# The last pair ahead of the first inverse's products, and the bonus taken out of PSUM by ScalarE, in an SGU / RWKV-7 trunk

## The chip, the cores and the metric

The kernel runs on one core of one Trainium2 chip. The core has a matrix engine (TensorE, "PE" in the profile, with its weight loads shown apart as "PEld"), VectorE ("DVE"), ScalarE ("ACT"), GpSimd ("POOL") and SyncE ("SP"). Each engine takes its instructions from a queue of its own, in order. The metric is the device time of one execution in microseconds (us): the median of several runs of the kernel. One more execution was profiled; it gives the trace.

## The reference: what is computed

The input is 512 tokens of 1024 channels. Two residual layers follow each other. Layer 0 mixes tokens with a spatial-gating unit (SGU), layer 1 with RWKV-7 time mixing; each is followed by a gated convolutional FFN of width 2816, and a last RMSNorm ends the program. The change lies in layer 1 alone, whose mixer is, cut to what matters:

```python
r, k, v = xr @ w_r, xk @ w_k, xv @ w_v
kk = normalised(k * k_k) ; k = k * (1 + (a - 1) * k_a)
# per head (16 heads of 64), for each token t:
#   S = S diag(w_t) + (S a_t) b_t^T + v_t k_t^T ;  y_t = S r_t
y = wkv7_scan(r, decay, k, v, -kk, kk * a)
y = group_norm(y) * ln_w + ln_b
bonus = sum(r * k * r_k, per head) * v
out = ((y + bonus) * g) @ w_o
```

## The kernel before, in words

**Layout.** Activations lie with channels on the 128 partitions and the 512 tokens along the free dimension; 1024 channels are eight such tiles, which for the RWKV layer are called *pairs* (a tile holds two heads). Every dense product in fp32 is made of three products of rounded halves (mm3, L325 to L327): each k-tile costs three matmuls of 128x512.

**The chunked scan.** The recurrence is cut into eight chunks of 64 tokens. For each chunk and head a 64x64 triangular system must be inverted, and the matrices that enter it are made beforehand. The work of the layer is therefore split into streams, written as Python generators, each of which emits a bit of work and yields:

- `projections` (L808): the dense products for k, then for v, eight tiles each. In this part of the program one step makes two k-tiles of one output tile, that is six dense matmuls. Behind each v tile a generator `value` (L859) does the rest for it: it centres v through the PE (L868) and writes it out (L873, L874), and it makes the bonus: a product of r*k with a block matrix that holds r_k (L883), a multiplication by v (L885), and a ScalarE pass that adds the bias ln_b (L886). The product's PSUM bank is one of two of the tag "mm", which the dense products of the same stage also use (for the last tiles it is "aux"), and the bank is free again when L885 has read it.
- `pairs`: for each of the eight pairs, decay and operands (VectorE and ScalarE), and then `products` (L959): small matmuls into the banks "aux" and "us" (L973, L988), masked by VectorE (L977), copied by ScalarE (L978, L991) and written to DRAM for the scan. The first half of a pair's chunks is one step, the second half with L988 another.
- `invert(g)` (L1027): the inverses for pairs 4g to 4g+3, all chunks at once. ScalarE (for g = 1 partly VectorE) copies the 32x32 diagonal blocks (L1044, L1046), VectorE transposes them (L1051), solves row by row (rows j = 1 to 30, two dependent VectorE instructions each, L1069 and L1070; two rows to a step), and transposes the result twice, to z and to y. Then the off-diagonal blocks: first-stage products from z on the PE (L1090), copies of y by ScalarE (L1098), copies of the products (L1103), second-stage products from y (L1093) and their copies (L1105).
- `scan(g)`: the chunks in order, each a chain of small matmuls and copies (L1301 to L1329), with `finish` for the group norm, which adds the bonus from rt, and `gate` (L1203), which multiplies by the gate (L1209) and splits the result for the output projection.

**What sets the order.** The streams are woven by hand. `weave(main, side, fill, rate, lag, side_rate)` steps `main`; after each step it draws the dense stream `fill` at `rate` steps per main step, and the inverse (`side`) at `side_rate`. The tuple RATES holds these numbers per stage. `issue_after(ins)` orders what is emitted inside behind `ins` on the same engine; `step(gen, engines)` steps a generator behind the last instruction so far on the engines named. Everything that is not ordered this way or by data may be placed earlier in an engine's queue by the compiler.

Around the change the order of emission is: a stage in which the pairs 4 to 6 and the first half of pair 7 are the main stream, with the first inverse at 2.2 steps per main step (RATES[1]); then these lines:

```python
load(0, 0)
ahead = invert(1)
next(ahead)
self.weave(main, inv, fill, *RATES[4], ktiles=STEPS[1])
for _ in inv:
    next(fill)
    self.step(ahead, (mybir.EngineType.PE,))
```

that is, the second inverse's first input copies, the rest of pair 7 together with the first inverse, and what is left of that inverse with one dense step and one step of the second inverse each. Then comes `scan(0)`, with the second inverse as side stream. In `invert`, one dense step is drawn between the transposes z and y of the first inverse.

Of the kernel before, what the change touches and what calls it, by code (L numbers as in the profile page):

```python
# [12 lines left out]
F32 = mybir.dt.float32  # L13
F32R = mybir.dt.float32r
AF = mybir.ActivationFunctionType
ALU = mybir.AluOpType
# [4 lines left out]
P = 128  # L21
D = 1024
KT = 8
T = 512
# [5 lines left out]
GN_EPS = 64e-5  # L30
C1 = -0.5 * math.exp(-0.5)

RATES = ((1.9, 2), (1.9, 6, 2.2), (0.66, 2, 1.15), (0.72, 2), (1.2, 6, 2.2))
LEAD = 1
WB = 4
FIRST0, WAIT, STEPS = 1, 1, (2, 2, 2, 2)
# [108 lines left out]
class Emit:  # L145
# [622 lines left out]
    def rwkv_main(self, r, ctx, gain):  # L768
        nc, tc, A = self.nc, self.tc, self.A
        V, S, G = nc.vector, nc.scalar, nc.gpsimd  # L770
# [5 lines left out]
        ip = r.ip  # L776
# [31 lines left out]
        def projections():  # L808

            load = Ahead([lambda n=n, m=m: self.parts(n, m) for n in PARTS for m in range(KT)])  # L810

            def key(m, a):
                while m >= NKEY and m - NKEY not in used:
                    yield
                ks[m] = tmp("key", NKEY, T)
                S.copy(ks[m], a)

            for m in range(KT - 2):
                a = self.acc("mm")
                yield from self.dense_steps(a, load.take(), r.xk)  # L820
                yield from key(m, a)
                yield

            ws = [load.take(), load.take(False)]
            accs = [self.acc("mm") for _ in range(2)]
            xv = []
            for k in range(KT):
                for j in range(2):
                    self.mm3(accs[j], self.wcols(ws[j], k * P, P), r.xk[k], k == 0, k == KT - 1)
                while len(xv) < min(k + 3, KT):  # L830
                    xv.append(r.mix(3, len(xv)))
                if k == 4:
                    load.fetch()
                yield
            for j in range(2):
                yield from key(KT - 2 + j, accs[j])
            late = iter(())
            for m in range(KT):
                a = self.acc("mm")
                w = load.take()  # L840
                if m == KT - 2:
                    ga["w"] = load_gate(0)
                for n, _ in enumerate(self.dense_steps(a, w, xv)):
                    yield
                    next(late, None)
                    if m == KT - 1 and n == 0:
                        gw[0] = gate_weights(ga["w"])
                        ga["parts"] = self.gate_parts()
                    if m == KT - 1 and len(gx) < 2:
                        gx.append(gate_mix(len(gx)))  # L850
                for _ in late:
                    yield
                v = ip.tile([P, T], F32, tag="v", bufs=1, name=self.uid("v"))
                S.copy(v, a)
                late = value(m, v)
            next(late)
            tail.append(late)

        def value(m, v):  # L859
            g, i = divmod(m, 4)  # L860

            def bank():
                return self.acc("mm" if len(done) < KT else "aux")

            vt = ip.tile([P, NCH, C], F32, tag="vt", bufs=1, name=self.uid("vt"))
            q = bank()
            for b in range(4):
                nc.tensor.matmul(q[:, b * P:(b + 1) * P], v[:, b * P:(b + 1) * P], self.c("center", P),  # L868
                                 start=True, stop=True)
            q4 = q.rearrange("p (b h f) -> p b h f", b=4, h=2)  # L870
            for hd in range(2):
                for par in range(2):
                    S.copy(vt[H[1 - hd], par::2, :], q4[H[par], :, hd, :])  # L873
            nc.sync.dma_start(vtd[:, :, m].rearrange("c p f -> p c f"), vt)  # L874
            yield
            yield

            while m not in done:
                yield
            wb = ip.tile([P, P], F32, tag="wb", bufs=1, name=self.uid("wb"))  # L880
            S.activation(wb, self.c("bones", P), AF.Copy, scale=self.p("r_k", m))
            q = bank()
            nc.tensor.matmul(q, wb, rt[g][:, i, :], start=True, stop=True)  # L883
            b = rt[g][:, i, :]
            V.tensor_tensor(b, q, v, ALU.mult)  # L885
            S.activation(b, b, AF.Identity, bias=self.p("ln_b", m))  # L886
            vdone.add(m)
            yield

# [137 lines left out]
        def invert(g):  # L1027
# [9 lines left out]

            x = blocks("ix")
            pr = ip.tile([P, 272], F32, tag="pr", bufs=1, name=self.uid("pr"))
            cut = 24 * g  # L1040
            for us in (slice(0, cut), slice(cut, 32))[1 - g:]:
                for rows, cols in Q:
                    if us.start and g == 1:
# [5 lines left out]
            def turn(out, src):  # L1049
                for bs in [slice(n, n + 8) for n in range(0, 32, 8)] if g == 1 else [slice(0, 32)]:  # L1050
                    V.transpose(out[:, bs], src[:, bs])  # L1051
# [6 lines left out]
            for j in range(1, 31):  # L1058
# [6 lines left out]
                else:  # L1065
                    a = tt[:, j, j + 1:32].unsqueeze(1).to_broadcast([P, j, ni])
                    b = tt[:, 0:j, j].unsqueeze(2).to_broadcast([P, j, ni])
                    q = pr[:, 0:ni * j].rearrange("p (c i) -> p c i", i=ni)
# [4 lines left out]

            z, y = blocks("ix"), blocks("li")
            turn(z.rearrange("p u t -> p t u"), tt)
            if g == 0:
                next(fill)
            turn(y.rearrange("p u t -> p t u"), tt.rearrange("p s t -> p t s"))
            yield
            off, own = blocks("off"), iter(Q)  # L1080
            for i in range(2):
# [22 lines left out]
                        else:  # L1104
                            S.copy(tg[b0, us, 32:64], ps[b0])  # L1105

        gx, tail = [], []

        def gate_mix(k):
            with ExitStack() as behind:  # L1110
# [92 lines left out]
        def gate(g, i, ts, q=None):  # L1203

            if q is None:
                q = self.acc("aux")[:, 0:ts.stop - ts.start]
                opening(g, i, ts, q)
            o = rt[g][:, i, ts]
            V.tensor_tensor(o, o, q, ALU.mult)  # L1209
            while len(outs[g]) <= i:  # L1210
                outs[g].append(tuple(self.xr.tile([P, T], F32R, tag=t, bufs=10, name=self.uid(t)) for t in ("mxh", "mxl")))
            oh, ol = (x[:, ts] for x in outs[g][i])
            S.copy(oh, o)
            V.tensor_tensor(ol, o, oh.bitcast(F32), ALU.subtract)
# [16 lines left out]
        def load(g, c):  # L1231
            while 4 * g + 3 not in vdone:
                next(fill)

            ps = slice(4 * g, 4 * g + 4)
            if g == c == 0:
                st = [t for _ in range(2) for t in (self.xr.tile([P, T], F32, tag=tag, bufs=10, name=self.uid(tag))
                                                    for tag in ("mxh", "mxl"))]
                bt = scratch("ss").rearrange("p (i a f) -> p i a f", i=4, a=2)
                vu = scratch("rb").rearrange("p (a i f) -> p a i f", a=2, i=4)  # L1240
                for i in range(4):
                    nc.sync.dma_start(st[i][:, 0:RW], std[g][c, :, i])
            else:
                t = tile_([P, 4 * RW], "st", SCAN)
                st = [t[:, RW * i:RW * i + RW] for i in range(4)]
                nc.sync.dma_start(t, std[g][c].rearrange("p i t -> p (i t)"))
                n = c % 2
                if n == 0 or g == 0 and c == 1:
                    two[:] = tile_([P, 2, 4, 2, C], "cbt", 2), tile_([P, 2, 2, 4, C], "vu", 2)
                    cs = slice(c, c + 2 - n)  # L1250
                    for hd in range(2):
                        nc.sync.dma_start(two[1][H[1 - hd], n:, hd], vtd[cs, H[1 - hd], ps].rearrange("c p i f -> p c i f"))
                    nc.sync.dma_start(two[0][:, n:].rearrange("p c i a f -> p c (i a f)"),
                                      btd[cs, :, ps].rearrange("c p i a f -> p c (i a f)"))
                bt, vu = (t[:, n] for t in two)
            for hd in range(2):
                if g == c == 0:
                    nc.sync.dma_start(vu[H[1 - hd], hd], vtd[c, H[1 - hd], ps])
                if c == 0:
                    G.memset(vu[H[hd], hd], 0.0)  # L1260
            if g == c == 0:
                nc.sync.dma_start(bt, btd[c][:, ps])
            chunks[g, c] = st, bt, vu
# [157 lines left out]
        main = pairs()  # L1421
# [3 lines left out]
            pass  # L1425
        self.weave(until(main, lambda: KT - 2 in done), inv, fill, *RATES[1], ktiles=STEPS[1])
        load(0, 0)
        ahead = invert(1)
        next(ahead)
        self.weave(main, inv, fill, *RATES[4], ktiles=STEPS[1])  # L1430
        for _ in inv:
            next(fill)
            self.step(ahead, (mybir.EngineType.PE,))
        ctx.close()
        ep = ctx.enter_context(tc.tile_pool(name="scan", bufs=1))
        inv = ahead
# [88 lines left out]
```

## Time and profile before

| | |
|---|---|
| median of 3 runs | 1244.42 us (1243.08 to 1244.78) |
| the profiled execution | 1245.55 us, of it 1243.7 us span |
| PE busy | 1226.8 us (99%), 7535 matmuls |
| PEld busy | 1000.2 us (80%) |
| VectorE busy | 851.1 us (68%) |
| ScalarE busy | 633.1 us (51%) |
| GpSimd busy | 81.4 us (7%) |
| mean granted TensorE clock | 0.996 of full speed |

The span is the time from the first to the last recorded instruction; the execution's own time is 1.85 us longer. The profile's page lists the engines' busy time, busy shares over 40 slices with the granted clock of the PE (PEclk), and the costliest groups of instructions. The trace behind it can be asked for a time line of an engine, for who waited for whom, and for busy times and clock by stretches. In a row of the time line stand the start, the duration, the engine, the line of the kernel, the operation, output<-input and the count; in square brackets behind it the engine's idle time before it and what ended it. Matmuls overlap, so a matmul's duration is longer than the distance to the next start.

### The profile page before, as it was taken

Reading aid. Unit: us, or ns where it says so; the run is one execution under the profiler, and the core shown is the slowest. Engines: PE = TensorE matmul, PEld = TensorE weight load, DVE = VectorE, ACT = ScalarE, POOL = GpSimd, SP = SyncE. Lnnn points to the kernel's source line nnn. Section 1 sums busy time; section 2 is a strip of 40 time slices with the busy share of each in tenths; the row PEclk is TensorE's granted clock in tenths of the full one; section 3 lists DMA queues with packets and bytes.
Section 4 is the critical chain, followed back from the end, with each engine's and each line's share of the span. In section 5 each row is a group of like instructions: output and inputs, shape, how many; then the busy total and the mean of one; then the engine's idle time right before and its main releaser. Section 6 shows DMA issues by size and latency. Waiting matters only on the chain.

```text
span 1243.7 us, 19411 instructions
## 1 busy us (share of the span) xinstructions
PE 1226.8 (99%) x7535; PEld 1000.2 (80%) x7535; DVE 851.1 (68%) x1418; ACT 633.1 (51%) x1089; POOL 81.4 (7%) x106
## 2 busy tenths in 40 slices
PE   9999999999999999999999999999999999999997
PEld 6878888888888888877887777778888888888886
DVE  5566578888876454675899698776777777872323
ACT  6544455555554343466787667424544444543232
POOL 1100200000000001000000013222000000000000
PEclk9999999999999999999999899999999999999999
DMA  7232457887556776326888797654223223333332
GB/s 273 94 105 82 132 180 246 246 249 241 192 172 193 220 226 196 109 81 182 220 242 237 188 280 233 219 171 135 85 102 102 90 97 102 97 88 104 97 93 81
DMA packets 125133, 201.65 MB, mean 162 GB/s; under 512 B 39857, under 2 KB 63153, under 8 KB 125041
## 3 DMA queue, kind: packets, MB, share of 16 engines
q10 hardware_dynamic: 38976, 112.87, 29.5%
q1 hardware_dynamic: 86064, 87.54, 22.6%
q8 instruction: 59, 0.97, 0.3%
q14 instruction: 34, 0.27, 0.1%
HBM read 152.93 MB, written 47.45 MB: 161 GB/s over the span
## 4 chain that ended last, share of the span: by engine, by line
PE 91%; DVE 4%; DMA 3%; ACT 1%; issue 0%; SPq 0%; POOL 0%; DVEq 0%; POOLq 0%; ACTq 0%
PE mm L325 9%; PE mm L327 9%; PE mm L326 9%; PE aux L325 6%; PE aux L326 6%; PE aux L327 6%; PE e L325 6%; PE e L326 6%; PE us L325 6%; PE e L327 6%; PE us L327 6%; PE us L326 6%; PE us L1314 1%; PE aux L973 1%; PE aux L988 1%; PE us L1321 1%
## 5 line engine op out<-in xcount | busy, mean ns | idle before, releaser
L237 ACT CAST w<-w 128x512 fp32r<-128x512 f32 x340 | 206.5, 611 | 359.8 <-PE aux L327 92.6
L238 DVE TENSOR_TENSOR w<-w,w 128x512 fp32r<-128x512 f32 x340 | 230.5, 680 | 180.2 <-ACT w L237 179.6
L325 PE MATMUL mm<-mxh,w 128*128 128x512 f32 x408 | 167.9, 412 | 2.7 <-DVE rt L885 2.6
L327 PE MATMUL mm<-mxh,w 128*128 128x512 f32 x408 | 161.1, 395 | 0.0
L326 PE MATMUL mm<-mxl,w 128*128 128x512 f32 x408 | 160.6, 394 | 0.0
L325 PEld LDWEIGHTS mm<-mxh,w 128*128 128x128 f32 x408 | 77.0, 189 | 22.8 <-DVE rt L885 3.3
L327 PEld LDWEIGHTS mm<-mxh,w 128*128 128x128 f32 x408 | 77.0, 189 | 17.1 <-issue 0.8
L326 PEld LDWEIGHTS mm<-mxl,w 128*128 128x128 f32 x408 | 77.1, 189 | 16.2 <-issue 1.7
L575 ACT ACTIVATE cv<-z,par 128x512 f32<-128x512 f32 x88 | 71.7, 817 | 26.5 <-DVE z L573 21.2
L325 PE MATMUL aux<-mxh,w 128*128 128x512 f32 x216 | 84.5, 391 | 0.0
L325 PE MATMUL us<-mxh,w 128*128 128x512 f32 x216 | 84.5, 391 | 0.0
L327 PE MATMUL aux<-mxh,w 128*128 128x512 f32 x216 | 84.2, 390 | 0.0
L326 PE MATMUL aux<-mxl,w 128*128 128x512 f32 x216 | 84.1, 389 | 0.0
L326 PE MATMUL us<-mxl,w 128*128 128x512 f32 x216 | 84.1, 389 | 0.0
L327 PE MATMUL us<-mxh,w 128*128 128x512 f32 x216 | 84.1, 389 | 0.0
L354 POOL TENSOR_TENSOR ss<-ss,sq 128x512 f32<-128x512 f32 x24 | 31.7, 1323 | 761.1 <-ACT sq L352 761.1
L325 PE MATMUL e<-mxh,w 128*128 128x512 f32 x208 | 81.4, 391 | 0.0
L326 PE MATMUL e<-mxl,w 128*128 128x512 f32 x208 | 81.1, 390 | 0.0
L327 PE MATMUL e<-mxh,w 128*128 128x512 f32 x208 | 81.0, 389 | 0.0
L576 DVE SCALAR_TENSOR_TENSOR cv<-z,par,cv 128x512 f32<-128x512 f32 x88 | 66.0, 752 | 19.5 <-ACT cv L575 19.5
L577 DVE SCALAR_TENSOR_TENSOR cv<-z,par,cv 128x512 f32<-128x512 f32 x88 | 66.0, 752 | 2.9
L325 PEld LDWEIGHTS aux<-mxh,w 128*128 128x128 f32 x216 | 40.5, 188 | 9.0 <-issue 0.5
(1113 smaller groups left out, 2555.2 us busy)
## 6 DMA issues: line engine op xcount, KB each, us to landing
w<-in_wup ACTq DMA_DIRECT2D x88, 512.0 KB, 3.7
w<-in_wdn ACTq DMA_DIRECT2D x32, 512.0 KB, 3.7
st<-std SPq DMA_DIRECT2D x15, 640.0 KB, 6.6
w<-wkd ACTq DMA_DIRECT2D x16, 512.0 KB, 5.1
w<-wvd ACTq DMA_DIRECT2D x16, 512.0 KB, 5.1
w<-wod ACTq DMA_DIRECT2D x16, 512.0 KB, 4.2
w<-in_wdn ACTq DMA_DIRECT2D x16, 384.0 KB, 3.3
w<-in_wsu ACTq DMA_DIRECT2D x8, 512.0 KB, 3.7
```

The source lines that it names most:

```text
L237: nc.scalar.copy(hi[r, :n], src)
L238: (lo_eng or nc.vector).tensor_tensor(lo[r, :n], src, hi[r, :n].bitcast(F32), ALU.subtract)
L325: mm(acc, wh, xh, start=first, stop=False)
L326: mm(acc, wh, xl, start=False, stop=False)
L327: mm(acc, wl, xh, start=False, stop=last)
L354: nc.gpsimd.tensor_tensor(self.ss, self.ss, self.sq, ALU.add)
L575: nc.scalar.activation(c, z[:, 2:], AF.Identity, scale=cw(2, i), bias=self.p("conv_b", l * 44 + i))
L576: nc.vector.scalar_tensor_tensor(c, z[:, 1:T + 1], cw(1, i), c, ALU.mult, ALU.add)
L577: nc.vector.scalar_tensor_tensor(c, z[:, 0:T], cw(0, i), c, ALU.mult, ALU.add)
L973: nc.tensor.matmul(qs[hd][:, c - ch.start, :], bk[H[hd], c, C * hd:C * hd + P], ar[H[hd], c, :], start=True, stop=True)
L988: nc.tensor.matmul(qs[hd][:, c, :], bk[H[hd], c, C * hd:C * hd + P], dg[H[hd], c, :], start=True, stop=True)
L1314: nc.tensor.matmul((us, ux)[hd][H[hd], 1, i, :], ti[g][H[hd], i, c, :], wt[H[hd], i, :], start=True, stop=True)
```

## The change

- RATES: the first inverse's rate in the stage of pairs 4 to 7 goes from 2.2 to 1.6; in the short stage behind it the inverse is no longer woven in.
- The last pair's second half is woven with the dense stream alone, and all steps of the first inverse that are left follow it. The dense step between z and y is gone. Once z and y are emitted, each further step of the first inverse is followed by one step of the second, and at the fifth two dense steps are drawn, behind the last PE instruction.
- The second inverse's first input copies come behind the last pair, behind ScalarE's last instruction; they cover two of four pairs instead of three, and VectorE copies the other two (cut 16 instead of 24).
- The bonus product is copied out of PSUM by ScalarE; VectorE multiplies the copy by v in place. The ScalarE pass that added the bias is gone: `gate` adds it with a three-operand VectorE instruction in place of the multiplication. The tile v has two buffers instead of one.

```diff
-RATES = ((1.9, 2), (1.9, 6, 2.2), (0.66, 2, 1.15), (0.72, 2), (1.2, 6, 2.2))
+RATES = ((1.9, 2), (1.9, 6, 1.6), (0.66, 2, 1.15), (0.72, 2), (1.2, 6))
...
-                v = ip.tile([P, T], F32, tag="v", bufs=1, name=self.uid("v"))
+                v = ip.tile([P, T], F32, tag="v", bufs=2, name=self.uid("v"))
...
             nc.tensor.matmul(q, wb, rt[g][:, i, :], start=True, stop=True)
             b = rt[g][:, i, :]
-            V.tensor_tensor(b, q, v, ALU.mult)
-            S.activation(b, b, AF.Identity, bias=self.p("ln_b", m))
+            S.copy(b, q)
+            V.tensor_tensor(b, b, v, ALU.mult)
             vdone.add(m)
...
-            cut = 24 * g
+            cut = 16 * g
...
             turn(z.rearrange("p u t -> p t u"), tt)
-            if g == 0:
-                next(fill)
             turn(y.rearrange("p u t -> p t u"), tt.rearrange("p s t -> p t s"))
+            turned.append(g)
             yield
...
-        gx, tail = [], []
+        gx, tail, turned = [], [], []
...
-            V.tensor_tensor(o, o, q, ALU.mult)
+            V.scalar_tensor_tensor(o, o, self.p("ln_b", 4 * g + i), q, ALU.add, ALU.mult)
...
         load(0, 0)
+        self.weave(main, None, fill, *RATES[4], ktiles=STEPS[1])
         ahead = invert(1)
-        next(ahead)
-        self.weave(main, inv, fill, *RATES[4], ktiles=STEPS[1])
+        self.step(ahead, (mybir.EngineType.Activation,))
+        behind = 0
         for _ in inv:
-            next(fill)
-            self.step(ahead, (mybir.EngineType.PE,))
+            if turned:
+                behind += 1
+                for _ in range(2 if behind == 5 else 0):
+                    with tc.issue_after(self.last(mybir.EngineType.PE)):
+                        next(fill)
+                self.step(ahead, (mybir.EngineType.PE,))
```

## The prediction

> **What bounds the kernel now.** I read the page first, to see which engine the time belongs to.
>
> ```profile
> PE 1226.8 (99%) x7535; PEld 1000.2 (80%) x7535; DVE 851.1 (68%) x1418; ACT 633.1 (51%) x1089; POOL 81.4 (7%) x106
> ...
> PEclk9999999999999999999999899999999999999999
> ```
>
> The PE is busy for 1226.8 of 1243.7 us. No matmul is removed or added, so the change can win only what the PE loses: 16.9 us of idle time in the whole span, and time at a low clock. PEclk has one digit below 9, in the 23rd slice (684 to 715 us), which is where pair 7 and the first inverse's products lie. Next I asked who kept the PE waiting between 640 and 870 us, the stretch whose order changes:
>
> ```profile
> PE mm L325 <- DVE rt L885: 2.6, 2, 2.3
> PE us L1314 <- DVE wt L1304: 1.0, 2, 0.8
> PE us L1301 <- issue: 0.8, 1, 0.8
> PE e L923 <- ACT sq L913: 0.7, 1, 0.7
> PE e L899 <- DVE kn L950: 0.6, 1, 0.6
> ...
> PE e L1090 <- DVE ix L1051: 0.2, 1, 0.2
> ```
>
> (us in total, times, longest.) The largest is a dense product that waits for L885, the bonus multiplication: 2.6 us, of it 2.3 at once. Then the stretch around it, by windows (per engine busy us and count; the third number from the end is the granted clock):
>
> ```profile
> 660.00:680.00 20.00, 19.44 (x179) 15.97 (x178) 19.86 (x46) 15.01 (x31) 0.11 (x1) 1.00 0.86 226
> 680.00:694.00 14.00, 13.65 (x106) 10.58 (x105) 13.55 (x34) 5.40 (x13) 0.61 (x2) 1.00 1.02 286
> 694.00:696.00 2.00, 0.71 (x4) 0.23 (x2) 1.86 (x7) 1.39 (x3) 0.00 (x0) 1.00 0.80 171
> 696.00:698.00 2.00, 1.01 (x4) 0.86 (x5) 1.86 (x7) 1.03 (x2) 0.00 (x0) 0.99 0.99 288
> 698.00:700.00 2.00, 1.81 (x15) 1.27 (x15) 2.00 (x2) 0.89 (x2) 0.00 (x0) 0.50 0.60 181
> 700.00:702.00 2.00, 2.00 (x36) 1.94 (x32) 1.48 (x1) 0.48 (x1) 0.00 (x0) 0.50 0.21 81
> 702.00:704.00 2.00, 2.00 (x7) 1.61 (x7) 0.00 (x0) 1.95 (x5) 0.00 (x0) 0.50 0.00 0
> 704.00:706.00 2.00, 2.00 (x9) 1.51 (x7) 0.00 (x0) 1.96 (x3) 0.00 (x0) 0.80 0.52 108
> 706.00:724.00 18.00, 18.00 (x331) 14.41 (x330) 11.88 (x30) 14.62 (x27) 1.27 (x2) 1.00 0.71 187
> ```
>
> VectorE is full from 660 to 700 (19.86 of 20, 13.55 of 14), ScalarE is not (5.40 of 14). The PE stands still in the middle of it, and behind that gap its clock is halved from 698 to 704 and at 0.80 to 706. A matmul at half clock still counts as busy, so this loss is not in the idle time: 6 x 0.50 + 2 x 0.20 = 3.4 us of PE work. The place itself, on the PE, VectorE and ScalarE:
>
> ```profile
> 690.81 0.50 PE L325 MATMUL mm<-mxh,w 128*128 128x512 f32 x1
> ...
> 692.30 1.02 PE L883 MATMUL mm<-rt,wb 128*128 128x512 f32 x2
> ...
> 696.99 0.50 PE L325 MATMUL mm<-mxh,w 128*128 128x512 f32 x1 [2.28 <-DVE rt L885]
> ...
> 699.72 1.07 PE L1090 MATMUL e<-ix,ti 32*32 32x32 f32 x32 [0.19 <-DVE ix L1051]
> ...
> 707.33 1.20 PE L1090 MATMUL e<-ix,ti 32*32 32x32 f32 x64
> ```
>
> ```profile
> 692.77 0.68 DVE L977 TENSOR_TENSOR lq<-us,cst 128x512 f32<-128x512 f32 x1
> ...
> 696.25 0.68 DVE L885 TENSOR_TENSOR rt<-mm,v 128x512 f32<-128x512 f32 x1
> ...
> 697.67 1.99 DVE L1051 STREAM_TRANSPOSE ix<-li 128x1024 f32<-128x1024 f32 x1
> 699.51 1.97 DVE L1051 STREAM_TRANSPOSE li<-li 128x1024 f32<-128x1024 f32 x1
> ```
>
> ```profile
> 693.49 0.40 ACT L978 COPY ti<-lq 64x256 f32<-64x256 f32 x1 [0.44 <-DVE lq L977]
> 693.91 0.59 ACT L991 COPY bt<-aux 128x512 f32<-128x512 f32 x1
> 694.40 0.59 ACT L991 COPY bt<-us 128x512 f32<-128x512 f32 x1
> 695.01 0.40 ACT L881 ACTIVATE wb<-cst,par 128x128 f32<-128x128 f32 x1
> 696.97 0.73 ACT L886 ACTIVATE rt<-rt,par 128x512 f32<-128x512 f32 x1 [1.55 <-DVE rt L885]
> 697.05 0.53 ACTq L248 DMA_DIRECT2D w<-wvd  x1
> 697.60 0.56 ACT L854 COPY v<-mm 128x512 f32<-128x512 f32 x1
> ```
>
> The bonus product is complete at 692.30 + 1.02 = 693.32. VectorE reads its bank only at 696.25, behind rows of the first inverse, and the next dense product, which needs that bank, stands from 694.71 to 696.99.
>
> **The change part by part.** *Bonus.* Each of eight values loses a ScalarE pass (L886, 0.73) and gains a ScalarE copy out of PSUM; its nearest row is L854, same shape from the same banks, 0.56. VectorE still multiplies, 0.68 as L885, but the bank no longer waits for it. For the value at 692.30 the copy could run from 693.32 (ScalarE is between the two L978), and at the latest where L886 stands now but without its wait for VectorE, behind L991 and L881: from 695.41. So the bank is free between 693.9 and 696.0, and the gap shrinks from 2.28 to something between 0 and 1.3. I take 0: the copy stands ahead of the wb of the next value (L881) in the program's order, and the copies L978 and L991 around it end at 694.99 only if all precede it. The smaller wait of the same kind, 2.6 - 2.3 = 0.3, goes too. Gain 2.6, bounds 1.3 and 2.6. What is late next is the masks of pair 7 (L977) and rows, which no dense product waits for. The multiplication now waits for ScalarE; behind it on VectorE stand rows, and nobody on the PE. With two buffers the next v may be copied before the multiplication is done.
>
> *Clock.* The clock was 1.00 through the gaps of 0.7 and 0.6 us in the windows up to 680 and fell behind the one of 2.28. Without the gap I take the whole 3.4 us back; bounds 0 and 3.4. The Trainium skill (TensorE: Matmul & The Clock Gate, "Why this matters for your kernels") says that the PE may idle for some 3 us between bursts before its clock is halved; this trace shows the halving behind 2.28 us, so the measurement decides. By that rule the halving would have another cause and would not go with the gap; that is a rival below.
>
> *Order of the dense steps.* Counting yields: stage 0 and the start use 41 dense steps, the stage of pairs 4 to 7 takes floor(1.9 x 9) = 17. Before: one more between z and y, two with the last pair, one in the loop. After: two with the last pair, two at the fifth step. Four either way; the scan starts from the same dense step, and its draws and its filler matmuls (L1124) stay as they are. PE work 0.
>
> *Last pair first.* At 1.6 the stage takes floor(14.4) = 14 inverse steps instead of 19, that is rows up to 27; rows 28 to 30, z, y and all products are emitted behind pair 7. The rows are not tied to the PE and VectorE stays full, so they should still end near 697, and z and y near 701.5 (699.51 + 1.97). Without the gap and the low clock the PE works off pair 7 and the two dense steps (1.49 each, 690.81 to 692.30) first, and comes to the first products at about 709. Cover of z: some 7 us. Without it the PE would wait at most for z, 1.99, plus what is left of y. The products are 2 x 128 small matmuls, 1.20 per 64: 2.4 us a stage, as before. The 0.19 wait for z goes: gain 0.2.
>
> *Two dense steps between the product stages.* The second stage needs the copies of the first (L1103). These rows price ScalarE:
>
> ```profile
> L1098 ACT COPY ti<-li 32x1024 f32<-32x1024 f32 x8 | 8.3, 1043 | 2.7 <-DVE li L1051 2.6
> ...
> L873 ACT COPY vt<-mm 64x256 f32<-64x256 f32 x20 | 7.3, 366 | 0.3
> ...
> L1103 ACT COPY off<-e 32x512 f32<-32x512 f32 x4 | 2.3, 578 | 0.1
> ```
>
> The last two copies L1103 take 1.2 us; two dense steps are 3.0. But ScalarE must in that stretch also do four L1098 (4.2), four input copies of the second inverse (32x512 now, as L1103: 2.3), four L873 (1.5) and the other two L1103 (1.2): 10.4 in all, against four dense steps (6.0), the first stage (2.4), a bonus product and a centring (0.5 to 1.0 each): about 10 us of PE. It fits if at least one L1098 runs as soon as y is there at 701.5, ahead of the last pair's copies. I take a wait of 0; bounds 0 and 2.
>
> *Second inverse.* Ten of its steps instead of two are emitted before the scan, so rows up to 15 can be through when the scan starts, and fewer of them stand in front of the scan's wt copies (L1304), which cost the PE 1.0 us. VectorE copies 32 instead of 16 blocks per partition; nobody on the PE waits there. I take 0; bounds -1.0 and +1.0.
>
> *Bias in the gate.* A three-operand instruction for a two-operand one:
>
> ```profile
> L238 DVE TENSOR_TENSOR w<-w,w 128x512 fp32r<-128x512 f32 x340 | 230.5, 680 | 180.2 <-ACT w L237 179.6
> ...
> L576 DVE SCALAR_TENSOR_TENSOR cv<-z,par,cv 128x512 f32<-128x512 f32 x88 | 66.0, 752 | 19.5 <-ACT cv L575 19.5
> ```
>
> At most 0.07 us for each of eight tiles, 0.6 in all on VectorE, and no PE wait above names the gate: 0. No DMA is added; pair 7's writes on SP's queue only come earlier.
>
> *Sum.* 2.6 + 3.4 + 0.2 = 6.2; I take 6.0, 0.2 being left for short waits that move. The profiled execution took 1245.55, 1.13 above the median of 1244.42. So 1239.55 for such an execution, and 1238.4 for the median.
>
> **The rivals.** *1. A new gap at the first inverse's products.* Emitted last, with the two dense steps tied behind them, the products or their second stage find nothing to hide z, y or ScalarE's copies. For it: ScalarE's 10.4 against 10 above. Against it: y at 701.5 and 0.8 us at most in any other PE wait here. A gap of 2 us, with the clock halved again (3.4), costs 5.4: gain 0.6, 1243.8. A gap of 1 without it: 1239.4, which I count with the forecast.
>
> *2. The gap shrinks only.* The copy stands behind both L991 and L881: 1.3 us stay, and the clock falls for half as long (1.7): gain 3.2, 1241.2.
>
> *3. The halving is not the gap's doing* (the rule above): gain 2.8, 1241.6. For it only the rule; against it, that it begins within a microsecond of the gap's end and nowhere else in the stretch.
>
> *4. Slower: ScalarE becomes the late releaser.* The copy stands in ScalarE's queue behind copies that themselves wait for VectorE's masks, as L978 does at 693.49 and as longer queues would do. Then the gap and the halving stay, and each of the eight bonuses holds its bank for a ScalarE copy more, 0.56: up to 4.5, I take 3.5: 1247.9. It decides from the point where the queue ahead of the copy lasts longer than one dense step (1.49 us) behind the product. Against it: ScalarE's 5.40 of 14.
>
> **How the numbers follow.** Forecast 0.60, rival 1 0.14, rival 2 0.10, rival 3 0.05, rival 4 0.11. A measurement of this kernel can tell about 0.2%, 2.5 us, from no change. Faster: forecast, rivals 2 and 3, less 0.03 for forms of them that stay under 2.5 us: 0.72. Within 0.2%: rival 1 and those 0.03: 0.17. Slower: rival 4, 0.11. The low end adds the 1.0 of the scan's wt waits and 0.9 of the other short waits to the sum: 1236.5. The high end takes in rivals 2, 3 and 1 with a little more than its price: 1244.8; rival 4 and the worst forms of 1 are left out.
>
> **What would show it.** Right: no row "mm L325 <- DVE rt L885" among the PE's waits; clock 1.00 in every 2 us window from 680 to 730; the copy at most 1 us behind the bonus product; L973 of pair 7 ahead of every L1090 on the PE; PE idle time in 640 to 870 smaller by over 2 us. Wrong: a PE wait for L1098, L1103 or the transposes L1051 of over 1 us near 705 to 720, a clock of 0.50 anywhere behind it, or dense products that wait for the ScalarE copy.

## The result, and the profile after

The kernel after takes 1252.57 us (median of 4 runs, 1250.63 to 1255.47) against 1244.60 us (1243.08 to 1245.11) of the kernel before: a ratio of 1.0065, 95% interval 1.0048 to 1.0082. It is slower by 8 us where 6 us of gain were forecast. Its profiled execution took 1250.63 us, of it 1248.5 us span (before: 1245.55 and 1243.7). From L1078 on, line numbers of the kernel after are one less than those of before.

The page first (busy us of each engine; the granted clock in 40 slices):

```profile
PE 1225.8 (98%) x7535; PEld 998.1 (80%) x7535; DVE 852.1 (68%) x1418; ACT 631.5 (51%) x1089; POOL 81.5 (7%) x106
...
PEclk9999999999999999999999999999999999999999
```

The 8 in the clock row is gone, and the PE is busy 1.0 us less. The span grew by 4.8, so the PE stands still 5.8 us more. By windows (per engine busy us and count, then clock, DMA share, GB/s):

```profile
694.00:696.00 2.00, 1.99 (x9) 1.33 (x8) 1.87 (x6) 1.98 (x5) 0.00 (x0) 1.00 0.71 160
696.00:698.00 2.00, 2.00 (x15) 1.79 (x14) 1.86 (x7) 0.40 (x1) 0.00 (x0) 1.00 1.02 244
698.00:700.00 2.00, 2.00 (x17) 1.47 (x18) 1.90 (x4) 0.00 (x0) 0.00 (x0) 1.00 0.96 273
...
702.00:704.00 2.00, 0.57 (x2) 0.30 (x2) 0.10 (x1) 1.93 (x6) 0.00 (x0) 1.00 0.60 177
...
740.00:760.00 20.00, 16.66 (x358) 13.52 (x355) 16.56 (x44) 9.44 (x18) 7.29 (x8) 1.00 0.75 234
760.00:780.00 20.00, 17.34 (x301) 12.10 (x301) 13.14 (x25) 16.54 (x33) 1.91 (x4) 1.00 0.61 183
840.00:860.00 20.00, 19.05 (x127) 15.26 (x124) 11.85 (x35) 4.99 (x14) 1.83 (x5) 1.00 0.35 114
```

The same view of before, for the last three stretches:

```profile
740.00:760.00 20.00, 19.80 (x272) 14.43 (x273) 19.02 (x51) 9.85 (x23) 5.84 (x8) 1.00 0.85 274
760.00:780.00 20.00, 19.04 (x469) 14.89 (x465) 16.28 (x31) 19.39 (x34) 8.31 (x10) 1.00 0.77 222
840.00:860.00 20.00, 19.94 (x103) 16.10 (x99) 12.16 (x33) 7.10 (x17) 3.85 (x7) 1.00 0.47 152
```

The gap at 694 to 697 and the halved clock behind it are gone as forecast. A new hole of 1.4 us opens at 702.2. The loss is in the scan: 3.1 us of PE time more are idle in 740 to 760, 1.7 in 760 to 780, 0.9 in 840 to 860. Who keeps the PE waiting from 640 to 900 us (us in total, times, longest):

```profile
PE mm L883 <- ACT vt L873: 1.4, 1, 1.4
PE us L1313 <- DVE wt L1303: 1.3, 3, 0.5
PE us L1300 <- PE e L1325: 1.3, 2, 0.7
PE aux L1089 <- DVE ix L1051: 1.2, 1, 1.2
PE mm L1134 <- ACT mxh L237: 1.1, 2, 0.8
PE aux L1362 <- DVE y L1356: 1.0, 2, 0.8
PE mm L325 <- ACT mxh L1212: 1.0, 1, 1.0
```

No single row replaces the 2.6 us of before. There are seven of 1.0 to 1.4 us, all but the first in the scan, the second inverse or the gate. ScalarE's timeline around 757 us (start, us, engine, line):

```profile
754.23 2.10 ACT L1097 COPY ti<-li 32x1024 f32<-32x1024 f32 x2 [1.14 <-DVE li L1051]
756.34 1.50 ACT L873 COPY vt<-aux 64x256 f32<-64x256 f32 x4
757.87 1.17 ACT L1102 COPY off<-aux 32x512 f32<-32x512 f32 x2
759.05 1.04 ACT L1097 COPY ti<-li 32x1024 f32<-32x1024 f32 x1
760.11 0.72 ACT L1113 ACTIVATE sq<-h,par 128x512 f32<-128x512 f32 x1
```

In before the mix of that place (L1114 there) and the first gate product (L1135 there) were:

```profile
747.44 0.72 ACT L1114 ACTIVATE sq<-h,par 128x512 f32<-128x512 f32 x1
...
754.22 0.50 PE L1135 MATMUL mm<-mxh,w 128*128 128x512 f32 x1
```

The PE's timeline after, where the second inverse's products begin and where the first gate product runs, is:

```profile
753.80 0.69 PE L1089 MATMUL aux<-ix,ti 32*32 32x32 f32 x32 [1.15 <-DVE ix L1051]
...
761.01 0.50 PE L1134 MATMUL mm<-mxh,w 128*128 128x512 f32 x1
```

The scan began 2.9 us earlier than before (722.95 against 725.8). But with ten steps done ahead, the second inverse reaches its products at 753.8, not at 760.7, and its copies (L1097, L1102) stand ahead of the second gate mix (L1113) in ScalarE's order. The mix, which ran at 747.44 before, runs at 760.11, and the first gate product, the dense work that fills the scan there, at 761.0 instead of 754.2.

### The profile page after: what moved, and what is told of

Same layout as the page of the kernel before. It is cut to its first block, busy times and chain, and to the rows that moved or that the text cites. A ratio compares the mean times of both kernels' runs of the same rounds, so it can differ in the third digit from the quotient of the medians.

```text
span 1248.5 us, 19411 instructions
## 1 busy us (share of the span) xinstructions
PE 1225.8 (98%) x7535; PEld 998.1 (80%) x7535; DVE 852.1 (68%) x1418; ACT 631.5 (51%) x1089; POOL 81.5 (7%) x106
## 4 chain that ended last, share of the span: by engine, by line
PE 89%; DVE 5%; ACT 2%; DMA 2%; issue 1%; POOL 0%; SPq 0%; ACTq 0%; DVEq 0%; POOLq 0%
PE mm L325 9%; PE mm L327 9%; PE mm L326 9%; PE aux L325 6%; PE aux L326 6%; PE aux L327 6%; PE e L325 6%; PE us L325 6%; PE e L326 6%; PE e L327 6%; PE us L327 6%; PE us L326 6%; DVE pr L1069 1%; DVE li L1070 1%; PE aux L988 1%; PE aux L973 1%
## 5 line engine op out<-in xcount | busy, mean ns | idle before, releaser
L325 PE MATMUL mm<-mxh,w 128*128 128x512 f32 x408 | 166.9, 409 | 1.7 <-ACT mxh L1212 1.0
L325 PEld LDWEIGHTS mm<-mxh,w 128*128 128x128 f32 x408 | 76.6, 188 | 21.7 <-issue 2.3
L325 PE MATMUL aux<-mxh,w 128*128 128x512 f32 x216 | 84.5, 391 | 0.0
L325 PE MATMUL us<-mxh,w 128*128 128x512 f32 x216 | 84.5, 391 | 0.0
L325 PE MATMUL e<-mxh,w 128*128 128x512 f32 x208 | 81.5, 392 | 0.0
L325 PEld LDWEIGHTS aux<-mxh,w 128*128 128x128 f32 x216 | 40.6, 188 | 9.1 <-issue 0.5
```

The costliest lines, as they stand in the source:

```text
L325: mm(acc, wh, xh, start=first, stop=False)
```

## The experiments

Ahead of the first runs three theories stood. T1: the order of the ten steps costs the time. T2: ScalarE's copy releases the bonus bank late. T3: the last pair's place in front of the first inverse's products costs it. T4 came up on the way. Each kernel ran beside the kernel before (1244.0 to 1244.7 us); in short diffs, "-" is what the named starting kernel has.

**The bonus edit alone.** Start: before.

```diff
-            V.tensor_tensor(b, q, v, ALU.mult)
-            S.activation(b, b, AF.Identity, bias=self.p("ln_b", m))
+            S.copy(b, q)
+            V.tensor_tensor(b, b, v, ALU.mult)
...
-            V.tensor_tensor(o, o, q, ALU.mult)
+            V.scalar_tensor_tensor(o, o, self.p("ln_b", 4 * g + i), q, ALU.add, ALU.mult)
```

> The kernel before with the bonus edit alone: ScalarE copies the bonus product out of PSUM, two buffers for v, the bias in the gate; the order of everything else is that of before. Theory T1 (the loss is made by the order: eight more steps of the second inverse are emitted ahead of the scan, so the second gate mix, which is tied behind the last ScalarE and VectorE instruction, falls behind that inverse's copies): faster than before, 1238 to 1241 us, no wait of mm L325 for the bonus multiplication of over 1 us, clock 1.00 from 690 to 710, the second gate mix within 3 us of 747. Rival T2 (ScalarE releases the bonus bank late, in the scan above all): slower than before, 1248 or more. Rival T3 (the last pair's place ahead of the first inverse costs the time): about 1239, as T1.

Measured: 1248.69 us (1246.40 to 1251.72), ratio 1.0036 (1.0024 to 1.0048). T1's number (1238 to 1241) is missed, T2's (1248 or more) is met. The PE's waits in this kernel:

```profile
PE us L1314 <- DVE wt L1304: 3.1, 2, 1.8
PE e L1090 <- DVE ix L1051: 2.2, 1, 2.2
PE mm L325 <- ACT rt L885: 1.5, 2, 1.3
PE mm L325 <- ACT mxh L1213: 1.0, 1, 1.0
```

and ScalarE at the old gap:

```profile
694.97 0.58 ACT L991 COPY bt<-aux 128x512 f32<-128x512 f32 x1
...
695.45 0.59 ACT L991 COPY bt<-us 128x512 f32<-128x512 f32 x1
695.93 0.60 ACT L885 COPY rt<-mm 128x512 f32<-128x512 f32 x1
```

The copy stands behind both L991, as rival 2 had it, and 1.3 of the 2.28 us stay. In the profiled execution the clock did not fall. But what the PE wins here it loses fourfold further on: it stands 2.2 us for z, and later 3.1 for the scan's wt. In before these two waits were 0.2 and 1.0, so 4.1 us are lost against 1.0 of the gap. The wait for z:

```profile
698.72 1.90 DVE L1051 STREAM_TRANSPOSE ix<-li 128x1024 f32<-128x1024 f32 x1
...
700.68 0.69 PE L1090 MATMUL e<-ix,ti 32*32 32x32 f32 x32 [2.23 <-DVE ix L1051]
```

z is ready at 698.72 + 1.90 = 700.62, in before at 699.66. VectorE's rows lie 1.05 us later in this trace than in before already at 659 us, and so they do at 696; set against these rows, z comes at the same time as in before.

**The order alone.** Start: after, with the two bonus lines, the gate line and the single v buffer of before.

> The changed kernel with the bonus as it was before (VectorE multiplies out of PSUM, ScalarE adds the bias, one buffer for v). T1: still slower than before, 1249 to 1256 us, with the second gate mix on ScalarE behind the second inverse's copies at 755 us or later. T2: faster than before or equal, at most 1245. T3: slower than before, as T1.

Measured: 1251.03 us (1249.60 to 1252.27), ratio 1.0054 (1.0042 to 1.0066). This is T1's number, and T3's too. So each half alone is slower, by 4.7 and by 7.0 us, and together they cost 8.0: less than the sum.

**Two steps ahead instead of ten.** Start: after.

```diff
-                self.step(ahead, (mybir.EngineType.PE,))
+                if behind == 1:
+                    self.step(ahead, (mybir.EngineType.PE,))
```

> The changed kernel, but after the second inverse's first two steps the loop over the first inverse steps it no further, so that ten steps become two, as before. Last pair, dense steps and bonus stay as changed. T1: 1237 to 1241 us, the second gate mix on ScalarE near 745 us and ahead of the second inverse's copies, PE idle time between 740 and 780 under 2.5 us (6.0 in the changed kernel). T2: slower than before, 1248 or more. T3: slower than before, 1248 or more.

Measured: 1247.94 us (1245.94 to 1248.81), ratio 1.0024 (1.0011 to 1.0036). 4.6 of the 8.0 us come back, and the first gate product is at 753.4 again; but T1 had expected all of it, 1237 to 1241.

**The gate mixes untied.** Start: after; the tie of a gate mix behind the last VectorE and ScalarE instruction emitted is taken out.

> The changed kernel with the gate mixes no longer tied behind the last VectorE and ScalarE instruction; nothing else. T1: at least 5 of the 8 us come back, 1238 to 1247 us, with the second gate mix ahead of the second inverse's copies. T2 and T3: no difference from the changed kernel within 2 us, 1250 to 1255.

Measured: 1254.56 us (1253.47 to 1255.90), ratio 1.0085 (1.0071 to 1.0098). T1's form of that moment, that the tie itself is the cost, fell. Without it four mixes have started by 750.63, ahead of the second inverse's copies (from 760.06), and still the first gate product comes only at 767.5 and the kernel is no faster; the second inverse's first products now wait 2.5 us for z.

**The products in other banks.** Start: after.

```diff
-                    ps = self.acc("aux" if g == 1 else "e").rearrange("p (u t) -> p u t", t=32)
+                    ps = self.acc("e").rearrange("p (u t) -> p u t", t=32)
```

> The kernel after, with the second inverse's products in the two banks of tag e instead of the two of tag aux, in which the last v tiles' value sums and the finish's transposes also take their turn. T1 as it now stands (ten steps ahead put the products in front of that value work, and the shared banks make it queue behind their waits; some 7 us lost between 748 and 785): the first gate matmul, at 761.0 after and 754.2 before, comes back to 754 to 757, and the time falls by 3 to 6 us to 1246.5 to 1249.5. Rival (the steps' vector and scalar work in front of the gate mixes is the cost, whatever the banks): the first gate matmul stays at 760 to 762 and the time at 1251.5 to 1253.5. T3 (the last pair's place costs): as the rival.

Measured: 1252.24 us (1250.41 to 1255.22), ratio 1.0056 (1.0043 to 1.0070). The time is the rival's: the shared banks are not it. The first gate product was missed by both sides: it came at 750.5, earlier than in before, but the one for the next tile only at 768.1, and the time stayed. So the place of the first gate product does not tell the time by itself.

**The gate's bias alone, the pair order alone, the copy without the gate.** Starts: before, with the bias pass gone and the gate's line as above; the two-step kernel with the bonus of before; the two-step kernel with the bias pass back behind copy and multiplication.

> The kernel before with the bias moved into the gate's three-operand instruction alone: ScalarE's bias pass behind the bonus goes, VectorE's multiplication out of the bonus bank stays. If the gate's 1.0 us wait at about 850 in the two profiles with that instruction is its price: a wait of TensorE of 0.9 to 1.1 us at 845 to 855 and a time of 1244.8 to 1246.0 beside 1244.0 to 1244.6 of before. If the bias edit is hidden: 1243.8 to 1244.6. T2 (what cost 4.7 us in the bonus edit is ScalarE's copy as the late releaser) wants most of the 4.7 us to be missing here: at most 1.5 us above before; should this kernel be 3 us or more slower, T2 falls and the gate is the cost.

> The last pair in front of the first inverse's products, with the copy cut at 16 and the dense work drawn as in the kernel after, but the second inverse taken two steps ahead of the scan as in before, and the bonus as in before. T1: the order costs nothing by itself once the ten steps are two, so 1243.0 to 1245.0 beside 1244.0 to 1244.6, and the 3.4 us that the kernel with two steps and the new bonus stood above before are the bonus edit's. T3 (the pair's place costs): 1246 to 1249, with new waits of TensorE of over 1.5 us in all between 680 and 744.

> The kernel with two steps ahead of the scan and the new order, with ScalarE's copy out of the bonus bank kept, but the bias back in its pass on ScalarE and the gate's product with two operands. If the gate's three-operand instruction costs the 1.0 us seen at about 850: that wait is gone and the time is 0.7 to 1.2 us below the 1247.9 of the same kernel with the bias in the gate, 1246.7 to 1247.2. T2 (the copy is the late releaser, and a pass more on ScalarE makes it later): 1247.5 to 1249.5, with the wait for the bonus tile of 0.5 us or more. If neither costs: 1243 to 1245.

Measured: 1249.16 us (1248.24 to 1252.14), ratio 1.0036 (1.0024 to 1.0048); 1244.08 us (1243.54 to 1245.40), ratio 0.9995 (0.9986 to 1.0003); 1249.78 us (1247.78 to 1250.13), ratio 1.0035 (1.0023 to 1.0047). T3 fell: the pair order is free. T2 had set its own end, a gate alone that costs 3 us or more, and 4.8 is beyond it: ScalarE's copy is not the whole cost of the bonus edit. In the third kernel the gate's wait at 850 is gone, but the time is not the 1246.7 to 1247.2 expected for that; it lies just above T2's 1247.5 to 1249.5. The bonus edit became a riddle: the gate without the copy costs 4.8 us, the copy without the gate 5.7 beside the same order, both together no more. Two edits that share no instruction cost the same. In the profile of the last one no wait of the PE between 640 and 900 us is over 1.9 us, but the clock is low for long (windows):

```profile
760.00:762.00 2.00, 0.78 (x24) 0.42 (x17) 2.00 (x5) 1.36 (x2) 0.00 (x0) 1.00 0.86 307
762.00:764.00 2.00, 1.74 (x31) 1.44 (x33) 1.94 (x4) 1.96 (x4) 1.57 (x2) 0.85 0.72 267
764.00:766.00 2.00, 2.00 (x41) 1.43 (x38) 1.49 (x3) 1.19 (x2) 0.00 (x0) 0.50 0.01 4
...
774.00:776.00 2.00, 2.00 (x5) 1.11 (x4) 0.00 (x0) 1.94 (x5) 0.42 (x1) 0.50 1.03 411
```

What the two edits may share is that the compiler puts other instructions in other places once an engine's work changes. In before, ScalarE's vu copy of the scan's fifth chunk stands ahead of the copies L873 and two gate mixes:

```profile
757.57 0.37 ACT L1316 COPY vu<-us 64x256 f32<-64x256 f32 x1 [1.13 <-PE us L1314]
758.61 1.50 ACT L873 COPY vt<-aux 64x256 f32<-64x256 f32 x4 [0.67 <-PE aux L868]
760.01 1.33 ACT L1114 ACTIVATE sq<-h,par 128x512 f32<-128x512 f32 x2
```

In the next kernel (bias in the gate, the pass kept as a plain copy) it comes behind one L1098, the copies L873 and a mix:

```profile
758.45 1.04 ACT L1098 COPY ti<-li 32x1024 f32<-32x1024 f32 x1 [2.78 <-DVE li L1051]
759.50 1.50 ACT L873 COPY vt<-aux 64x256 f32<-64x256 f32 x4
760.91 0.72 ACT L1114 ACTIVATE sq<-h,par 128x512 f32<-128x512 f32 x1
761.66 0.37 ACT L1316 COPY vu<-us 64x256 f32<-64x256 f32 x1
```

The gate alone has the same order, and its PE waits 2.3 us for vu. The vu copy is a link of the scan's chain: L1321, L1326 and the next chunk wait for it. T4: such places are the cost. The copy without the gate speaks against it as the whole answer: its vu copy stands behind L873 and one mix, but so it does in the pair order alone (at 756.92 and 757.20), which is as fast as before.

**The pass kept, and the bias twice.** Starts: before. The first is the kernel just described (gate line as above, `S.copy(b, b)` in place of the bias pass); the second has the gate line alone, so that ln_b is added twice.

> The kernel before with the bias in the gate's three-operand instruction, and ScalarE's pass behind the bonus kept as a plain copy in place, so that no instruction is taken from any engine. New theory T4, formed after the gate alone cost 4.8 us: what costs is neither the gate nor the copy, but where the compiler puts instructions in the queues once an engine's work changes. In the compiled order of this kernel, as in that of the gate alone, ScalarE has one L1098, the copies L873 of a v tile and a gate mix L1114 ahead of the scan's vu copy L1316 that stands first among them in before (at 757.57 us). T4: 1247 to 1250, with a wait of TensorE for vu of over 1 us at 755 to 765. Rival (the pass that went, or the loads that came earlier for it, is the cost): 1244.5 to 1246.0, that is before and the gate's 1.0.

> The kernel before with the three-operand instruction in the gate and nothing else changed: ScalarE's bias pass stays as well, so the bias is added twice. The compiled order of every engine is that of before up to the first gate product at about 845 us. T4 and everybody who holds the gate for cheap: the wait of 1.0 us at about 850 is the whole price, 1244.9 to 1246.0 beside 1244.3. Rival (the gate's instruction is the cost of the gate alone): 1248 to 1250.

Measured: 1249.62 us (1248.04 to 1253.85), ratio 1.0044 (1.0029 to 1.0059), with a PE wait of 2.5 us for vu, as T4 had it; and 1246.51 us (1244.14 to 1250.15), ratio 1.0011 (0.9999 to 1.0023). With the same gate instruction and the old places the edit costs 1.8 us or, by its interval, next to nothing; with a plain copy and the new places 4.9. In the traces the plain copy takes 0.62 us and the pass 0.72, so the copy's own time is not what costs.

**Ten steps ahead, products late.** Starts: after, and the order alone.

```diff
-RATES = ((1.9, 2), (1.9, 6, 1.6), (0.66, 2, 1.15), (0.72, 2), (1.2, 6))
+RATES = ((1.9, 2), (1.9, 6, 1.6), (0.66, 2, 0.6), (0.72, 2), (1.2, 6))
```

> The kernel after, ten steps of the second inverse ahead of the scan, but with the rate of that inverse beside the scan at 0.6 steps a main step instead of 1.15, so that its first products are emitted at the 15th main step as in before (17 / 1.15 = 14.8 there, 9 / 0.6 = 15 here) and not at the 8th (9 / 1.15 = 7.8). T1 as it now stands (the place of the products and their copies among the value work and the gate mixes costs, not that the rows come early): first gate matmul back from 761.0 to 752 to 756, last value product on aux back from 769.5 to 755 to 760, and 1245.5 to 1248.5, as with two steps ahead (1247.9) or less. Rival (ten steps of row work ahead of the scan on VectorE are the cost): 1250.5 to 1253.

> The same order and rate (ten steps ahead, 0.6 beside the scan) with the bonus of before. T1 with T4: the order costs nothing once the products come late and the bonus is not touched, 1242.5 to 1245.5; the version most likely to beat both. Rival (the ten steps): 1249 to 1252.

Measured: 1250.71 us (1246.35 to 1256.29), ratio 1.0044 (1.0029 to 1.0059); and 1247.23 us (1246.14 to 1252.90), ratio 1.0025 (1.0014 to 1.0036). By its median the first kernel lies in the rival's range, 1250.5 to 1253; the second lies between the two. The milestones moved as T1 said: the first gate product is at 753.6 and, in the second kernel, at 750.9. The runs scatter with the clock. Those of mean clock 0.998 and above are 1246.4 us (median of 5) and 1247.0 (of 9); the kernel after has two such runs, 1250.63 and 1250.76, and the order alone has three of 1249.60 to 1251.71. So the late products are worth some 4 us at whole clock, by few runs; by the medians it is 1.9 and 3.8. The clock is no neutral ground either, since a kernel's own waits may lower it. The order with ten steps still stands some 3 us above the one with two (1244.08), so T1's number for the second kernel is missed, and why stays open.

**One queue place.** Start: before; no instruction is changed.

```diff
-                S.copy(vu[h1, 1], ux[h1, 1])
+                with ExitStack() as kept:
+                    if (g, c) == (0, 4):
+                        kept.enter_context(tc.issue_after(self.last(mybir.EngineType.Activation)))
+                    S.copy(vu[h1, 1], ux[h1, 1])
```

> The kernel before, not one instruction changed; only ScalarE's vu copy (L1316) of the scan's fifth chunk is ordered behind the ScalarE instruction emitted ahead of it. In the compiled order it then stands behind the copies L873, a gate mix and one L1098, as in the slow kernels with the bonus edit, and a few queue places that follow from it move too. T4 (the placement is the cost): 1247 to 1250, TensorE waiting over 1 us for vu at 755 to 765. Rival (the placement goes with the edits but costs nothing by itself): 1244 to 1245.5.

Measured: 1249.00 us (1247.20 to 1250.75), ratio 1.0031 (1.0019 to 1.0042). ScalarE's rows in before stand above (757.57 to 760.01). In this kernel (the vu copy is L1319 here):

```profile
757.92 1.50 ACT L873 COPY vt<-aux 64x256 f32<-64x256 f32 x4 [2.16 <-PE aux L868]
759.33 0.72 ACT L1114 ACTIVATE sq<-h,par 128x512 f32<-128x512 f32 x1
759.95 1.03 ACT L1098 COPY ti<-li 32x1024 f32<-32x1024 f32 x1
760.88 0.61 ACT L237 CAST mxh<-sq 128x512 fp32r<-128x512 f32 x1
761.52 0.37 ACT L1319 COPY vu<-us 64x256 f32<-64x256 f32 x1
```

and the PE in this kernel:

```profile
761.55 0.49 PE L1135 MATMUL mm<-mxh,w 128*128 128x512 f32 x1 [2.57 <-ACT mxh L237]
761.97 0.69 PE L1324 MATMUL us<-vu,cbt 128*64 128x64 f32 x16
```

The copy comes at 761.52 instead of 757.57, the chain's product L1324 at 761.97 instead of 759.60 (L1321 in before), and the PE stands 2.6 us. The row names the gate mix, not vu as expected: the gate product is first in the PE's queue, and the chain's product, which filled this time in before, is late for vu. 4.3 us come out of one position in ScalarE's queue and the few that follow from it, with no instruction changed. A part of them may be clock: behind the new wait it stands at 0.50 from 764 to 766, and all seven runs have a mean clock of 0.994 to 0.996. The eight runs of before beside them with 0.996 or 0.997 have a median of 1245.8 us, which leaves 3.2.

**One dense step less ahead of the scan.** LEAD is 0 instead of 1, in the bonus edit alone, in before and in the pair order with two steps. Then the vu copy stands in front of L873 in all three.

> The bonus edit alone, with the one dense step that is drawn ahead of the scan left to a later draw. In the compiled order the vu copy of the fifth chunk then stands ahead of the copies L873 and the gate mix again, and ScalarE's order in the scan is that of the kernel before with the same draw left out, which runs beside it. T4: the edit costs at most the gate's 1.0 us there, and its closed gap (2.28 us to 1.3) may win 1: ratio to that kernel between -1.0 and +1.2 us. Rival (the bonus edit costs its 4.4 us wherever things are placed): 3.5 to 5.5 us above it.

> The kernel before without the dense step drawn ahead of the scan: the control for the bonus edit with that draw left out. One dense step of 1.49 us is drawn later; all theories: 1243 to 1247, nearer to before.

> The last pair first with two steps ahead of the scan and the old bonus (1244.1, no low clock), with the dense step ahead of the scan left to a later draw, which puts the vu copy of the fifth chunk ahead of the value copies, where the other had a wait of 1.2 us for it. T4: that wait goes, 1242 to 1244, unless the scan's start waits for the missing dense step; rival (a wait for vu there is covered anyway): 1243.8 to 1245.5.

Measured: 1253.66 us (1250.19 to 1254.84), ratio 1.0066 (1.0051 to 1.0082); 1250.62 us (1249.15 to 1254.75), 1.0049 (1.0034 to 1.0064); 1248.74 us (1247.38 to 1249.54), 1.0028 (1.0017 to 1.0039). The draw itself costs 6.0 us in before and 4.7 in the pair order, which no theory expected; in all three the PE has a new 1.9 us wait, "mm L325 <- issue". The bonus edit costs 3.0 us between the first two, between T4's 1.2 and the rival's 3.5: not settled. In its profile the waits for z (2.2 against 0.8) and wt (2.4 against 1.6) are longer again, and a finish transpose waits 1.2 for the bonus copy (L1363 for L885), which is T2 in the small. The pair order's number was missed by both sides (1242 to 1245.5). No version beats both kernels; the pair order with two steps is not to be told from before.

## Why the prediction was wrong

**What was right.** The gap at 694 to 697 and the clock of 0.50 behind it went. In the kernel after, the copy L885 runs at 694.89 and the next dense product does not wait for it in that place. The pair order is free (1244.08 us), the dense steps between the products cost nothing, and the gate's instruction is 0.06 to 0.07 us longer than the old one, as taken (two of them 0.61 against 0.48).

**Second inverse: the step that failed most.** "I take 0; bounds -1.0 and +1.0." Two steps in place of ten give back 4.6 us, and ten steps with late products some 4 at whole clock. I asked only who waits for the input copies and the rows. I did not follow the inverse to its end: eight steps gained ahead of the scan bring its products 7 main steps forward (9 / 1.15 = 7.8 instead of 17 / 1.15 = 14.8), onto the last values and the gate mixes. The products' copies now stand ahead of the mixes on ScalarE, and the PE has less dense work to put between the links of the scan. That the place of the products costs is shown by the two steps, and by the late products at whole clock; that it costs by way of the mixes is not. With the mixes untied they were early, with other banks the first gate product was, and neither kernel was faster.

**Bonus.** 2.6 us were taken. The bonus edit alone leaves 1.3 of the gap, my lower bound, and loses 4.7 us in all. The premise failed, that the PE's idle time is a sum from which a gap can be subtracted. VectorE's rows, full to 700 us, set when z is there; a PE that arrives 2 us earlier, measured against these rows, waits 2 us more for it. That was in the rows I quoted ("19.86 of 20").

**Clock.** 3.4 us were taken as PE work won. Over four batches, 41 runs of the kernel before had a mean clock of 0.996 to 0.997 and a median of 1245.58 us, 33 had 0.998 to 0.999 and 1243.99: the runs with the low clock are 1.6 us longer. The pair order alone, whose trace has no low clock in this stretch, agrees with its 1244.08. That the rest of the 3.4 is covered by waits for other engines, as above, is likely but not shown. It isn't always so: in the copy without the gate, where the clock stays at 0.50 from 764 to 776, the PE is busy 5.5 us longer than in the same order with the old bonus (1230.2 against 1224.7), and the time is 5.7 longer.

**Bias in the gate.** I took 0. A dense product waits 1.0 us for the gate's split (L1213) at 850 in the profile of each kernel that has the instruction, except the one with the dense step left out; I looked only at waits that were there before. The bias twice costs 1.8 us by the medians, and 1.1 between runs of whole clock (1245.05, median of 5, against 1243.99).

**What no step had.** The compiler's places. The text said that what is not ordered may be placed earlier, and priced each edit as if everything else stayed where the trace had it. The kernel with one moved copy shows what such a place is worth: 4.3 us, nearly as much as either half of the bonus edit, and perhaps some of it by way of the clock. That the places carry most of the cost of the bias edit is shown by the pair of the pass kept and the bias twice (4.9 against 1.8). For the copy it is not shown. In the order with two steps nearly all of its 5.7 us is PE time at low clock, and the vu copy's place is that of the kernel beside it. In the old order, how much is the place, how much the longer waits for z and wt and how much the low clock stays open, since moving the places back also moved a dense step.

**The rivals.** Rival 2 gave the gap's length (1.3 us) but not the time. Rival 1's gap came, at 702.2 and 1.4 us long, because the copies L873 stand behind one L1097 that waits for y; the clock did not fall. Rival 4 had the sign and nearly the time of the bonus edit alone (1247.9), but only 1.3 us of the gap stayed, the clock did not fall in its trace, and no row shows the 0.56 us a bonus that it charged.

## What to carry to other kernels

When steps of a side stream are moved forward, follow the stream to its last step and see on what its products and copies now fall. A gap of the bottleneck engine is worth only what the engine it next waits for allows; if that one is full up to there, the gain is given back at the next wait. Where a compiler may reorder the queues, compare the compiled order of the two kernels before pricing an edit by its instructions: one copy of a serial chain behind its neighbours cost 4.3 us here, where the whole change was to win 6.0.

## What the runs showed of the hardware that was not expected

The length of a gap does not decide whether the clock is halved. It was halved behind a gap of 2.28 us (before) and behind one of 1.48 us with 0.7 us lost 5 us before (the copy without the gate, 0.50 for over 10 us), and stayed at 1.00 behind 2.23 us for z in the bonus edit alone and behind the 1.4 us at 702.2 in the kernel after. The plainest pair is the old gap itself: 2.28 us long in before and 2.29 in the kernel with the pass kept, where the clock behind it stayed at 1.00. The same kernel falls into it in some runs and, it seems, not in others: 41 of 74 runs of before have a mean clock of 0.997 or less, as the profiled one has. The Trainium skill (TensorE: Matmul & The Clock Gate, "Why this matters for your kernels") allows some 3 us of idle time; the halvings here came behind less.
